# Input projections of a hybrid attention layer: six tile pairs by seven block products, kept in DRAM for the attentions

## The chip, the cores and the metric

The kernel runs on one core of a Trainium2 chip. The metric is the device time of one execution in microseconds (us). Its engines work side by side: TensorE (PE, matmuls; PEld loads its weights), VectorE (DVE), ScalarE (ACT), GpSimd (POOL), and SyncE (SP), which issues most transfers. POOL issues transfers too, on a queue of its own. Each engine executes its own instructions in order and waits for others by semaphores. On-chip memory holds tiles of 128 partitions; products land in eight banks of 512 fp32 columns.

## The reference

One layer of a streaming encoder for 1024 prompt tokens and 32 sample tokens, in fp32:

```
h   = rms_norm(x) * (1 + scale1) + shift1            # scale1, shift1 from silu(c) @ w_ada
p   = h @ w_in    # 4256 columns: q_lat 384 | c_kv 256 | k_r 32 | q_b 512 | k_b 512 | v_b 512 | g_a 1024 | g_b 1024
o_a = latent attention (softmax)       o_b = stick-breaking attention of q_b, k_b, v_b
x   = x + gate1 * rms_norm((sigmoid(g_a) * (o_a @ w_proj_a) + sigmoid(g_b) * (o_b @ w_proj_b)) @ w_out)
x   = x + gate2 * rms_norm(conv_ffn(rms_norm(x) * (1 + scale2) + shift2))
```

The change is in `p = h @ w_in` and in what stands around the stick-breaking attention. k_b and v_b are outputs as well.

## The kernel before

An fp32 product is made of three matmuls: every operand is split into a rounded part (`hi`, on ACT) and the remainder (`lo`, on DVE), and `mm3` (L71) adds high x high, high x low and low x high. `h` lies on chip for the whole first half, transposed, as `Hh` and `Hl`: eight k-tiles of 128 rows by 1056 tokens. A **projection tile** is 128 columns of `w_in` for all tokens: three blocks of 352 tokens (`BLK`), eight k-tiles, three matmuls each, 72 in all.

`stage_h` loads x and the first two ada vectors of `w_ada` in halves (`ada_half`: 8 + 8 transfers of 512 KB), normalises and transposes. `stage_sb` then takes four pairs of heads in turn (`sb_pair`): it projects the pair's q, k and v tiles (`mtile`, evacuated into `Qe`, `Qo`, `KHe`, ..., `V`), sends k and v through transposes to the outputs, and runs the attention of the pair (`sb_attend`).

The attention's order on PE, ACT and DVE is written by hand in `ORDER`, one for all pairs; the tokens are executed as they stand. `S1.0` is the score of head and row block, `a` and `e` two sigmoids on ACT, `c` the running product (DVE scan), `x` a product on DVE, `T` the transposes of one square of weights (PE), `h` and `v` their rounded and low part (ACT, DVE), `V` the product with the values (PE), `o` and `p` the sum of a result (ACT, DVE). `f` is a **fill**: one k-tile of a gate projection (three matmuls), or one k-tile of a later ada vector. The gates come from the generator in `gates`: in each pair four tiles, 4 x (24 + 2) = 104 fills; `G` sends a gate block to DRAM, `W` and `w` split the next gate weight on ACT and DVE, `D` adds an ada sum. So all 16 gate tiles lie beside the four attentions, and the 12 tiles of q, k, v between them.

`stage_lat` projects the five latent tiles and the rope key from the same `Hh`, `Hl`, and the kernel goes on with the latent attention, the merge, the up projection (already with seven block products for each pair of tiles) and the down projection.

Of the kernel before, what the change touches and what calls it, by code (L numbers as in the profile page):

```python
# [17 lines left out]
P = 128  # L18
# [25 lines left out]

class K:
# [9 lines left out]
    BUFS = {"A": 5, "Q": 3, "big": 3, "o": 2, "QZ": 1, "t": 5, "mh": 4, "ml": 4, "dh": 3, "dl": 3, "ada": 1, "G": 1, "Gs": 1, "xs": 1, "jk": 1, "s": 3, "M": 2, "pv": 1, "tr": 2, "mm": 2, "KSm": 1, "VSm": 1, "ObH": 1, "ObL": 1}  # L55
# [97 lines left out]
    def late_vectors(self):  # L153

        nc, a = self.nc, self.a
        v = self.tl(self.At, [P, TP], F32, "A")
        ps = self.bank("tr")
        dma = nc.gpsimd.dma_start
        self.rows_T(ps, v[:13, 0:P], ((0, 8, a["g_pre_ffn"][0]), (8, 3, a["g_q_lat"][0]), (11, 2, a["g_kv_lat"][0])), dma)
        for w in range(6):  # L160
            x = a["conv_w"][0, w] if w < 3 else a["conv_b"][0] if w == 3 else a["state_ffn_conv"][0, 0, w - 4]
            self.rows_T(ps[:, 44 * (w + 1) :], v[:44, P * (w + 1) : P * (w + 2)], ((0, 44, x),), dma)
        nc.vector.tensor_copy(self.gvT[:, 8:21], ps[:, :13])
        nc.vector.tensor_copy(self.cvT.rearrange("p w c -> p (w c)"), ps[:, 44 : 44 * 7])

# [22 lines left out]

    def ada_step(self, n, pool, tp, late):


        nc, a = self.nc, self.a
        ps = self.bank("mm")
        for i, (v, k) in enumerate(self.ada_todo[:n]):
            if k == 0:
                self.acc = self.tl(tp, [P, 256], F32, "ada")
                for j in range(4):
                    c = v * D + j * 256
                    nc.sync.dma_start(self.acc[32 * j : 32 * j + 32], a["b_ada"][0, c : c + 256].partition_broadcast(32))
            w = self.tl(pool, [P, D], F32, "wr")  # L200
            nc.sync.dma_start(w, a["w_ada"][0, k * P : (k + 1) * P, v * D : (v + 1) * D])
            for j in range(4):
                nc.tensor.matmul(ps[32 * j : 32 * j + 32, :256], self.cT[:, k], w[:, j * 256 : j * 256 + 256],
                                 start=i == 0, stop=i == n - 1)
            if i < n - 1:
                yield
        acc = self.acc
        late.append(lambda: nc.vector.tensor_tensor(acc, acc, ps[:, :256], ALU.add))
        del self.ada_todo[:n]
        self.ada_sum = v if k == KT - 1 else None  # L210
        yield
# [28 lines left out]
    def ada_half(self, hf, wp, tp):  # L240
# [4 lines left out]
        for k in range(KT):  # L245

            last = hf == 1 and k >= KT - 2
            w = self.tl(*((self.W, [P, 1024]) if last else (wp, [P, 2 * 512])), F32, "wr").rearrange("p (v n) -> p v n", v=2)
            nc.sync.dma_start(w, a["w_ada"][0, k * P : (k + 1) * P].rearrange("p (v h n) -> p v h n", v=6, h=2)[:, 0:2, hf])
            for j in range(4):  # L250
                c = (j % 2) * 256
                nc.tensor.matmul(ps[32 * j : 32 * j + 32, :256], self.cT[:, k], w[:, j // 2, c : c + 256],
                                 start=k == 0, stop=k == KT - 1)
        nc.vector.tensor_copy(acc, ps[:, :256])
# [8 lines left out]
        self.gain(self.g1, 1, 0, 4 * hf, 4)  # L263


    def norm_T(self, t0, xs, g, sv, tp, k0=0, k1=KT):


        nc = self.nc
        if t0 < 8:  # L270
            n = len(xs) * P
            m = 512 // n
            c = slice(t0 * P, t0 * P + n)
            for k in range(k0, k1, m):
                tr = self.bank("tr")
                f = self.tl(tp, [P, 512], F32, "hf").rearrange("p (k c) -> p k c", k=m)
                for e in range(m):
                    kc = slice((k + e) * P, (k + e) * P + P)
                    for j, x in enumerate(xs):
                        o = e * n + j * P  # L280
                        nc.tensor.transpose(tr[:, o : o + P], x[:, kc], self.idt)
                h, l = self.Hht[:, k : k + m, c], self.Hlt[:, k : k + m, c]

                both = t0 == 4 and k0 == 0
                for e in range(m):
                    for x in (f, h) if both else (f,):
                        nc.scalar.activation(x[:, e], tr[:, e * n : e * n + n], AF.Identity,
                                             bias=self.adaT[:, sv, k + e, 0:1], scale=g[:, k + e, 0:1])
                if not both:
                    nc.vector.tensor_copy(h, f)  # L290
                nc.vector.tensor_tensor(l, f, h.bitcast(F32), ALU.subtract)  # L291
        else:
            tr = self.bank("tr")
            for c in range(2):
                nc.tensor.transpose(tr[:, c * P : c * P + P], xs[0][:, c * P : c * P + P], self.idt)
            f = self.tl(tp, [P, 512], F32, "hf")[:, :256].rearrange("p (k t) -> p k t", t=TS)
            for k in range(k0, k1):
                j, c = k // 2, k % 2
                nc.scalar.activation(f[:, k], tr[:, c * P + 32 * j : c * P + 32 * j + 32],
                                     AF.Identity, bias=self.adaT[:, sv, k, 1:2], scale=g[:, k, 1:2])  # L300
            f, h, l = (x[:, k0:k1] for x in (f, self.Hht[:, :, TP:T], self.Hlt[:, :, TP:T]))
            nc.vector.tensor_copy(h, f)
            self.lo(l, f, h)
# [22 lines left out]
    def new_H(self):  # L326
        self.Hp = self.tc.alloc_tile_pool(name=self.nm("H"), bufs=1, side="right", reuse_waits="tile")
        self.Hht = self.Hp.tile([P, KT, T], F32R, name=self.nm("hh"))
        self.Hlt = self.Hp.tile([P, KT, T], F32R, name=self.nm("hl"))
        self.Hh = [self.Hht[:, k] for k in range(KT)]  # L330
        self.Hl = [self.Hlt[:, k] for k in range(KT)]

    def stage_h(self):
        nc = self.nc
        self.new_H()
        a = self.a
        with self.tc.tile_pool(name="st_h", bufs=2, reuse_waits="tile") as tp, self.tc.tile_pool(name="wada", bufs=8, reuse_waits="tile") as wp:
# [3 lines left out]
            def load(t):  # L341
                x = self.tl(wp, [P, D], F32, "x")
                nc.sync.dma_start(x, a["x_prompt"][0, t * P : (t + 1) * P])
                nc.vector.tensor_scalar(x, x, self.rstd(self.sumsq(x, P, tp, "jk0", 1024), D, P), None, ALU.mult)
                xts.append(x)

            def norm(t, hf):
                self.norm_T(t, xts[t : t + 4] if t < 8 else [xs], self.g1, 0, tp, 4 * hf, 4 * hf + 4)

            for t in range(4):  # L350
                load(t)
            self.ada_half(0, wp, tp)
            norm(0, 0)
            w = [self.w_in_tile(672)]
            for t in range(4, 8):
                load(t)
            w.append(self.w_in_tile(672 + 512))
            self.in_w = w
            norm(4, 0)
# [3 lines left out]
            self.ada_half(1, wp, tp)  # L363
            nc.vector.tensor_scalar(xs, xs, self.rstd_s(xs, tp), None, ALU.mult)
            norm(0, 1)
            norm(8, 0)
            norm(4, 1)
            norm(8, 1)


# [9 lines left out]

    BLK = ((0, NB), (NB, NB), (2 * NB, NB))
# [10 lines left out]
    def to_natural(self, f, outs, ev):  # L392

        nc = self.nc
        for t0 in (0, 4, 8):
            tr = self.bank("tr")
            n = 4 if t0 < 8 else 1
            for j in range(n):
                r = P if t0 < 8 else TS
                nc.tensor.transpose(tr[:r, j * P : j * P + P], f[:, (t0 + j) * P : (t0 + j) * P + r], self.idt)  # L400
            ev(tr, t0, n, P if t0 < 8 else TS)

    def sb_pair(self, p):
        nc, a = self.nc, self.a
        q0, k0, v0 = 672 + p * P, 672 + 512 + p * P, 672 + 1024 + p * P

        Qe = self.tl(self.Sp, [P, TP], F32R, "Q")
        Qo = self.tl(self.Sp, [P, TP], F32R, "Q")
        wh, wl = self.w_in_tile(q0)
        for c0, n, ps in self.mtile(wh, wl, self.Hh, self.Hl, self.BLK, KT):  # L410
            m = min(n, TP - c0)
            c = slice(c0, c0 + m)
            self.hi(Qe[0:64, c], ps[0:64, :m], 0.125)
            self.hi(Qo[64:128, c], ps[64:128, :m], 0.125)
            st = nc.vector.scalar_tensor_tensor
            st(Qe[64:128, c], ps[0:64, :m], 0.125, Qe[0:64, c].bitcast(F32), ALU.mult, ALU.subtract)
            st(Qo[0:64, c], ps[64:128, :m], 0.125, Qo[64:128, c].bitcast(F32), ALU.mult, ALU.subtract)
            if m < n:
                nc.scalar.mul(self.qsb[:, p], ps[:, m:n], 0.125)

        KHe = self.tl(self.Sp, [P, TP], F32R, "KH")
        KHo = self.tl(self.Sp, [P, TP], F32R, "KH")
        KLe, KLo = self.KLz
        kf = self.tl(self.At, [P, BIG], F32, "big")
        wh, wl = self.w_in_tile(k0)
# [1808 lines left out]
```

## Time and profile before

| | us |
|---|---|
| median of 3 runs (1730.93 to 1736.36) | 1733.21 |
| the profiled execution | 1733.63 |
| its span, first to last instruction | 1731.5 |
| start, until PE is full | about 0 to 45 |
| first score of the four attentions | 83.10, 199.56, 321.94, 437.15 |
| latent projections and their norms | about 530 to 620 |

A row of a group gives line, engine, operation, output<-inputs, shape, count, then busy us and the mean ns of one, then the idle time before it and what ended it. A row of the timeline gives start, length, engine, line and operation. Ends of matmuls are modelled and overlap the next ones, so their rate is read from start to start.

### The profile page before, as it was taken

How to read it: one execution, taken by the hardware profiler on the slowest of the kernel's cores; microseconds unless marked ns; L12 is line 12 of the kernel's file. 1: busy time of each engine (PE TensorE's matmuls, PEld its weight loads, DVE VectorE, ACT ScalarE, POOL GpSimd, SP SyncE). 2: the span in 40 equal slices, each digit the busy share in tenths (PEclk: the TensorE clock that was granted, in tenths of full speed). 3: DMA queues.
4: the chain of work that ended last, by engine and by line, in shares of the span. 5: the costliest groups of instructions: out<-in, count | busy, mean ns of one | idle time of the engine just before them, and what ended most of it. 6: DMA issues, size and time to landing. Idle time of an engine off the chain costs nothing. (4 is left out here: it accounts for less than half of the span.)

```text
span 1731.5 us, 29721 instructions
## 1 busy us (share of the span) xinstructions
PE 1691.4 (98%) x11518; PEld 1542.4 (89%) x11518; DVE 1207.4 (70%) x1971; ACT 911.7 (53%) x1748; POOL 283.9 (16%) x586
## 2 busy tenths in 40 slices
PE   6999999999999999999999999999999999999998
PEld 3899999999999988989889789999999999977886
DVE  4576574673663687767786679887787787778456
ACT  5454453553554666766784286444444444544442
POOL 2211110211120011101100043211111121110013
PEclk8999999999999999999999999999999999999999
DMA  8343333333342222222345531534323323697743
GB/s 322 90 132 96 108 107 97 106 113 92 112 122 68 65 65 64 75 59 68 138 143 175 184 130 37 165 104 129 129 92 128 128 92 128 212 334 248 241 147 121
DMA packets 170093, 223.62 MB, mean 129 GB/s; under 512 B 12917, under 2 KB 117056, under 8 KB 169952
## 3 DMA queue, kind: packets, MB, share of 16 engines
q1 hardware_dynamic: 154336, 177.91, 32.4%
q0 software_dynamic: 15392, 43.74, 7.1%
q8 instruction: 90, 1.47, 0.4%
q14 instruction: 51, 0.42, 0.1%
q10 hardware_dynamic: 224, 0.09, 0.0%
HBM read 169.92 MB, written 51.25 MB: 128 GB/s over the span
## 5 line engine op out<-in xcount | busy, mean ns | idle before, releaser
L65 ACT ACTIVATE wh<-wr 128x1024 fp32r<-128x1024 f32 (+6 forms) x158 | 133.8, 856 | 249.6 <-PE s L1688 78.8
L68 DVE TENSOR_TENSOR wl<-wr,wh 128x1024 fp32r<-128x1024 f32 (+5 forms) x155 | 152.7, 991 | 139.6 <-ACT wh L65 139.0
L72 PE MATMUL mm<-hh,wh 128*128 128x352 f32 x688 | 231.6, 337 | 0.0
L73 PE MATMUL mm<-hl,wh 128*128 128x352 f32 x688 | 224.2, 326 | 0.4 <-DVE hl L291 0.3
L74 PE MATMUL mm<-hh,wl 128*128 128x352 f32 x688 | 224.2, 326 | 0.0
L72 PEld LDWEIGHTS mm<-hh,wh 128*128 128x128 f32 x688 | 130.0, 189 | 9.0 <-issue 4.9
L73 PEld LDWEIGHTS mm<-hl,wh 128*128 128x128 f32 x688 | 130.0, 189 | 3.9 <-DVE hl L291 1.8
L74 PEld LDWEIGHTS mm<-hh,wl 128*128 128x128 f32 x688 | 129.7, 189 | 0.8 <-issue 0.8
L68 DVE TENSOR_TENSOR PTl<-tr,PTh 128x512 fp32r<-128x512 f32 x100 | 68.3, 687 | 50.3 <-ACT PTh L65 49.9
L1689 PE MATMUL s<-T,wl 128*128 128x256 f32 (+1 forms) x328 | 93.6, 285 | 0.0
L1687 PE MATMUL s<-T,wh 128*128 128x256 f32 (+1 forms) x328 | 93.2, 284 | 0.0
L1688 PE MATMUL s<-T,wh 128*128 128x256 f32 (+1 forms) x328 | 93.2, 284 | 0.0
L1828 DVE SCALAR_TENSOR_TENSOR u<-u,c,u 128x1058 f32<-128x1058 f32 x68 | 87.0, 1317 | 2.0 <-ACT u L1825 0.7
L65 ACT ACTIVATE PTh<-tr 128x512 fp32r<-128x512 f32 x100 | 59.4, 598 | 53.5 <-PE tr L591 50.8
L591 PE MATMUL tr<-c,A 128*128 128x128 f32 x576 | 83.6, 274 | 0.6 <-DVE A L693 0.5
L1689 PE MATMUL tr<-T,wl 128*128 128x272 f32 (+1 forms) x272 | 77.6, 285 | 0.4 <-DVE wl L68 0.4
L1687 PE MATMUL tr<-T,wh 128*128 128x272 f32 (+1 forms) x272 | 77.9, 287 | 0.0
L1688 PE MATMUL tr<-T,wh 128*128 128x272 f32 (+1 forms) x272 | 77.5, 285 | 0.0
L68 DVE TENSOR_TENSOR wl<-S,wh 128x1024 fp32r<-128x1024 f32 x40 | 48.9, 1223 | 37.4 <-ACT wh L65 36.2
L591 PEld LDWEIGHTS tr<-c,A 128*128 128x128 f32 x576 | 68.1, 140 | 5.9 <-issue 1.6
L1689 PE MATMUL mm<-T,wl 128*128 128x256 f32 (+1 forms) x256 | 73.0, 286 | 0.3 <-DVE wl L68 0.2
L1687 PE MATMUL mm<-T,wh 128*128 128x256 f32 (+1 forms) x256 | 73.1, 286 | 0.0
(694 smaller groups left out, 5391.4 us busy)
## 6 DMA issues: line engine op xcount, KB each, us to landing
wr<-in_w_ada_dram SPq DMA_DIRECT2D x48, 512.0 KB, 4.6
wr<-in_w_up_dram SPq DMA_DIRECT2D x44, 512.0 KB, 4.2
dr<-in_w_down_dram SPq DMA_DIRECT2D x43, 512.0 KB, 5.9
wr<-in_w_in_dram SPq DMA_DIRECT2D x33, 512.0 KB, 4.6
wr<-gdn SPq DMA_DIRECT2D x30, 512.0 KB, 4.2
gdn<-u POOLq DMA_DIRECT2D x23, 512.0 KB, 5.3
gd<-nat POOLq DMA_DIRECT2D x48, 176.0 KB, 2.3
t<-gd SPq DMA_DIRECT2D x16, 528.0 KB, 6.3
```

What stands on the lines that cost most here:

```text
L65: self.nc.scalar.activation(out, in_, AF.Identity, scale=scale)
L68: return self.nc.vector.tensor_tensor(out, full, hi.bitcast(F32), ALU.subtract)
L72: m(ps, lh, rh, start=start, stop=False)
L73: m(ps, lh, rl, start=False, stop=False)
L74: self.pe = m(ps, ll, rh, start=False, stop=stop).ins
L591: self.nc.tensor.transpose(tr[:, (2 * s + q) * P : (2 * s + q + 1) * P], at[q][:, b * P : b * P + P], self.idt)
L1687: m(ps[:, :n], w[0][:, k], x[0][:, k, c], start=first and k == 0, stop=False, skip_group_check=True)
L1688: m(ps[:, :n], w[0][:, k], x[1][:, k, c], start=False, stop=False, skip_group_check=True)
L1689: i = m(ps[:, :n], w[1][:, k], x[0][:, k, c], start=False, stop=k == 3, skip_group_check=True)
L1828: nc.vector.scalar_tensor_tensor(y, u[:, w : w + YW], self.cvT[:, w, cc : cc + 1], y, ALU.mult, ALU.add)
```

## The change

The 1056 tokens are held in two halves of 528 (`HC`), each half of `h` in two halves of k (four k-tiles): blocks `B11`, `B21` (first half of the tokens) and `B12`, `B22`. A pair of weight tiles then is a 2 x 2 by 2 x 2 block product, computed by seven products of four k-tiles by 528 tokens instead of eight (steps a to g), with sums of the token blocks `T1` to `T4`, which are made once, and sums of the weights, made for each pair.

1. A new stage `stage_in` runs before the attentions. It projects all 12 q, k, v tiles and four gate tiles: two pairs (q and k of the first pair of heads, two gates) by plain products (`Plain`), begun in `stage_h` while the sums of tokens are made beside them, then six pairs by seven products.
2. Results go to DRAM (`z_done`): q and k split (`qhd`, `qld`, `khd`, `kld`), v transposed and split (`vd`), gates as before (`gd`). `sb_load` brings the operands of a pair back on SP's queue; `V` has one buffer, `KLz` one per head. The block `B12` goes to DRAM in `stage_h` and comes back at the end of `stage_in`, since `T4` takes its place in between.
3. `gates` runs once for 12 tiles, three beside each attention. Blocks are 4 x 264 (`HBLK`) instead of 3 x 352, also in `stage_lat`; ada steps are 3, 3, 2 for the three tiles: 3 x 32 + 8 = 104 fills for each pair. `ORDER` is written anew.
4. `stage_h` has a written order; ACT writes the rounded `h` and the full one, where DVE cast the rounded one before. Memsets of the attention's tables go from DVE to POOL.

```diff
+class Plain:
+    def go(self, half, b, tag, part=None):
...
+        for kh in range(2) if part is None else (part,):
+            k.z_half([x[:, 4 * kh : 4 * kh + 4] for x in self.w], k.B[kh][half], b, ps, kh == 0)
+        if part != 0:
...
+            k.nc.scalar.copy(self.u[:, half * HC + c0 : half * HC + c0 + n], ps[:, :n])
...
+    Z_BLK = ((0, 256), (256, 272))
...
+    def step_a(self, g, tags):
+        w = self.unit(g["ra"][:, :512])
+        g["q1"] = self.z_q("q1", 3)
+        self.z_out(g["q1"], self.z_prod(w, self.Z["B11"], tags))
...
+    def step_d(self, g, tags):
+        X = g["X"] = self.z_prod(self.unit(g["ra"][:, :512]), self.Z["T2"], tags)
+        g["q2"] = self.tl(self.Zp, [P, HC], F32, "q2", 2)
+        self.z_out(g["q2"], X, g["q5"])
+
+    def step_e(self, g):
+        self.z_prod(self.unit(g["rb"][:, :512]), self.Z["T3"], None, g["X"])
...
+    def step_f(self, g):
+        self.z_prod(self.unit(g["rb"][:, 512:]), self.Z["T4"], None, g["X"])
...
+    def stage_in(self):
...
+        for n in range(2, len(self.PAIRS)):
+            g = self.group(n)
+            self.raw_a(g)
+            self.raw_b(g)
...
+            self.step_a(g, "s s")
...
+            self.step_b(g, "s pv")
+            self.step_c(g, "s s")
+            while self.done:
+                self.z_done(*self.done.pop(0))
+            self.out_c(g)
+            self.sums_w(g)
+            self.step_d(g, "mm mm")
...
+            self.step_e(g)
+            self.step_f(g)
...
+            self.sum_4(g)
+            self.step_g(g, "s pv")
...
+    HBLK = tuple((264 * i, 264) for i in range(4))
...
+    def sb_load(self, p):
...
+            dma(KH[lo], kh[r])
+            dma(KH[hi], kh[r])
+            dma(KL[r], kl[r])
+            dma(Q[r], qh[r])
+            dma(Q[o], ql[r])
+            ops.append((Q, KH, KL))
+            if r is lo:
+                V = self.tl(self.Sp, [P, 8, 2, P], F32R, "V", 1)
+                dma(V, self.vd[p])
...
+        f S1.0 f a1.0 S0.0 f e1.0 c1.0 f a0.0 f e0.0 f x1.0 f c0.0 f x0.0 S0.1 f G a0.1 S1.1 e0.1 f c0.1
+        a1.1 f x0.1 f W c1.1 f T0.0 S2.0a e1.1 S2.0b w f h0.0 f a2.0a f a2.0b f v0.0 e2.0a x1.1 V0.0 e2.0b G
+        c2.0a T1.1 o0 T1.0 h1.1 p0 S2.1a h1.0 x2.0a S2.1b v1.1 a2.1a v1.0 a2.1b V1.1 e2.1a c2.0b V1.0 e2.1b
...
+        T7.1 V7.2 h7.1 f T7.0 v7.1 f h7.0 f V7.1 v7.0 f2 G D V7.0 f o7 f p7 f5 G
...
-                for b, (c0, n) in enumerate(self.BLK):
+                for b, (c0, n) in enumerate(self.HBLK):
+                    if b == 2:
+                        yield from self.ada_step((3, 3, 2)[i % 3], self.W, self.At, ada)
...
+        self.fill = self.gates(range(4, 16))
```

More of the change, by code (lines that the diff above doesn't have):

```diff
@@ L194, in ada_step @@
         for i, (v, k) in enumerate(self.ada_todo[:n]):
[L195 to L201, printed above, removed]
+            w = self.ada_w.pop() if self.ada_w else self.ada_load(pool, tp, i, v, k)
             for j in range(4):
@@ L263, in ada_half @@
         self.gain(self.g1, 1, 0, 4 * hf, 4)
-    def norm_T(self, t0, xs, g, sv, tp, k0=0, k1=KT):
-        nc = self.nc
-        if t0 < 8:
[L271 to L291, printed above, removed]
```

605 lines of the change are left out of this document (443 added, 162 removed).

## The prediction

> **What bounds the kernel now.** I read the page first, then the table of busy time by stretches, then the timeline of TensorE.
>
> ```profile
> span 1731.5 us, 29721 instructions
> ...
> PE 1691.4 (98%) x11518; PEld 1542.4 (89%) x11518; DVE 1207.4 (70%) x1971; ACT 911.7 (53%) x1748; POOL 283.9 (16%) x586
> ```
>
> TensorE (PE) is busy for 98% of the span, so a stage gets shorter by what PE is spared in it, as long as nothing else takes its place. The table of stretches says where that could happen; its columns are the stretch, its length, and busy time (with instructions) of PE, PEld, DVE, ACT and POOL, then granted clock, DMA share and GB/s.
>
> ```profile
> 321.94:399.60 77.66, 77.66 (x556) 73.11 (x555) 58.02 (x89) 42.65 (x94) 14.25 (x38) 1.00 0.40 122
> 399.60:437.15 37.55, 37.53 (x238) 36.95 (x236) 11.37 (x16) 12.79 (x24) 4.14 (x6) 1.00 0.27 78
> ...
> 620.00:860.00 240.00, 235.49 (x1653) 210.12 (x1652) 180.04 (x444) 169.89 (x422) 33.59 (x58) 1.00 0.23 71
> ...
> 1050.00:1506.00 456.00, 454.90 (x3793) 447.20 (x3792) 367.64 (x542) 222.37 (x362) 91.62 (x206) 1.00 0.36 119
> ```
>
> The first row is one stick-breaking attention (the third pair) with its four gate tiles beside it, the second the three projections q, k, v of the next pair. Both are full of PE work at clock 1.00. In the attention VectorE (DVE) works 58.02 of 77.66 us (75%). The third row, most of the latent attention, has DVE at 75% too, and PE idles 1.9%; the fourth, the up projection, which already uses seven block products, has DVE at 81% and PE idles 0.2%. So 75 to 81% of DVE can go with a full PE, and can cost 2%.
>
> **What a matmul costs.** Ends are modelled and overlap, so I count from start to start: 26 rows of 352 columns (first and last shown), 12 rows of 264, four transposes up to the next start, and, from the chain of waits, two marks three up-projection pairs apart.
>
> ```profile
> 399.88 0.33 PE L72 MATMUL mm<-hh,wh 128*128 128x352 f32 x1
> ...
> 403.96 0.32 PE L73 MATMUL mm<-hl,wh 128*128 128x352 f32 x1
> ...
> 645.38 0.29 PE L72 MATMUL mm<-ObH,wh 128*128 128x264 f32 x1
> ...
> 646.72 0.29 PE L74 MATMUL mm<-ObH,wl 128*128 128x264 f32 x1
> ...
> 394.22 0.60 PE L591 MATMUL tr<-c,A 128*128 128x128 f32 x4
> 394.57 0.72 PE L605 MATMUL pv<-ptd,V 128*128 128x256 f32 x4
> ...
> 1179.67 1.43 PE pv L1965 x24
> 1242.77 1.43 PE pv L1965 x24
> ```
>
> 352 columns: 4.08 us / 25 = 0.163 us. 264 columns: 1.34 / 11 = 0.122 us. Both are 0.46 ns a column, so a width of 264 carries no price of its own. A transpose of 128 columns takes 0.35 / 4 = 0.088 us, 0.028 more than that rate; such a floor exists, but below 264. A projection tile is 72 matmuls of 352: 11.75 us; two tiles are 23.5. A pair of tiles by seven block products takes (63.10 - 1.43) / 3 = 20.56 us.
>
> **The change part by part.**
>
> *Block products.* Six pairs (12 tiles) go from 23.5 to 20.56 us each: 6 x 2.94 = **-17.7 us**. Four tiles stay plain, in blocks of 256 and 272: 4 x 96 x 0.122 = 46.9 against 47.0, nothing. Their evacuation, the transposes to natural layout, the ada steps (32 in all before and after) and the late vectors are the same PE work, elsewhere.
>
> *Widths.* Twelve gate tiles and the latent tiles go from three blocks of 352 to four of 264: 96 x 0.122 against 72 x 0.163, nothing. By the Trainium skill, "TensorE: Matmul & The Clock Gate", section "Back-to-back issue gap", a stream of weight loads and matmuls takes 81 ns at 128 columns and 131 ns at 512, which has a large fixed part per matmul; the two rows above (0.163 and 0.122 us, proportional to the width) do not agree, and I go by the rows. The 504 more matmuls would cost about 32 us by the page's fixed part of 64 ns, an estimate from its two figures.
>
> *Start.* The first 60 us are no full PE:
>
> ```profile
> 35.00:40.00 5.00, 5.00 (x32) 2.99 (x30) 1.67 (x4) 3.72 (x7) 0.00 (x0) 0.71 0.58 224
> 40.00:45.00 5.00, 4.58 (x54) 2.53 (x53) 1.43 (x4) 0.24 (x2) 0.82 (x4) 1.00 0.00 2
> ...
> 43.08 1.50 PE L252 MATMUL s<-wr,cT 128*32 128x256 f32 x24
> ...
> 46.16 1.45 ACT L287 ACTIVATE hf<-tr,c,c 128x512 f32<-128x512 f32 x2 [5.93 <-DVE c L236]
> ...
> 56.10 1.18 ACT L299 ACTIVATE hf<-tr,c,c 128x32 f32<-128x32 f32 x4
> ...
> L73 PE MATMUL mm<-hl,wh 128*128 128x352 f32 x16 | 7.0, 435 | 0.4 <-DVE hl L291 0.3
> L72 PE MATMUL mm<-hh,wh 128*128 128x352 f32 x16 | 6.5, 409 | 0.0
> L74 PE MATMUL mm<-hh,wl 128*128 128x352 f32 x16 | 6.1, 378 | 0.0
> L72 PE MATMUL s<-hh,wh 128*128 128x352 f32 x14 | 4.6, 329 | 0.0
> L73 PE MATMUL s<-hl,wh 128*128 128x352 f32 x14 | 4.5, 323 | 0.0
> L74 PE MATMUL s<-hh,wl 128*128 128x352 f32 x13 | 4.3, 330 | 0.0
> ```
>
> Before, 89 projection matmuls of 352 (31.3 thousand columns) have started by 60 us. The new first stage issues 120 plain matmuls of 256 or 272: 31.3 thousand as well. The last ada weights have landed by 40 us (DMA share 0.00 behind it), but PE takes them at 43.08; the new order puts them ahead of the projections, which could bring the second half of the ada vectors 2 us earlier. Against it ScalarE (ACT) now writes both the rounded and the full value, 16 activations of 1.45 / 2 = 0.72 us after that point, with 2 x 1.18 for the sample and 3 copies: about 15 us from 44, so 59 to 60. I take **0**, bounds -4 (ada early, ACT never late) and +4 (PE held in the written order).
>
> *The new stage.*
>
> ```profile
> L68 DVE TENSOR_TENSOR wl<-wr,wh 128x1024 fp32r<-128x1024 f32 x4 | 4.8, 1212 | 2.8 <-ACT wh L65 2.8
> ...
> L208 DVE TENSOR_TENSOR ada<-ada,mm 128x256 f32<-128x256 f32 x4 | 1.7, 417 | 0.2 <-PE mm L203 0.2
> ```
>
> The sums of the tokens are eleven passes over two halves of 1056 columns (differences and low parts), at about 1.25 us (1.21 for 1024): 27 us of DVE beside 46.9 us of plain products; the plain tiles are their cover, and without it the first T2 product would wait. Within a group the same two banks are read by DVE between the products with T2, T3 and T4, with one bank's 12 matmuls (1.47 us) as cover for a read of 0.42 (the second row) plus whatever DVE is in, up to 1.2. The up projection has the same shape and lost 0.2%. Four such places in six groups: **+1.5**, bounds 0 and 5.
>
> *Spill and reload.* q, k, v go to DRAM and come back on SP's queue. Nothing of PE in that, but V has one buffer, so the load of the next V waits for the last value product, and behind it on SP stand the second head's operands and the next gate weight.
>
> ```profile
> wr<-in_w_up_dram SPq DMA_DIRECT2D x44, 512.0 KB, 4.2
> ...
> 20.00:25.00 5.00, 2.51 (x19) 1.56 (x19) 2.97 (x8) 3.23 (x4) 0.00 (x0) 0.93 1.05 404
> ```
>
> Behind that point lie 1.05 + 1.31 + 0.52 = 2.9 MB: 7.1 us at 404 GB/s, and 2.9 more to land (512 KB take 4.2, of which 1.3 at that rate): 10.0 us. The gate weight is split (W, on ACT) 19 fills later, with scores of 1.3 us and switches of about 0.5 between them: 19 x 0.366 + 1.8 = 8.8 us. ACT would wait 1.2 us; PE has six more fills and the scores S2.0 in hand before it needs ACT's h0.0. **+1** over three boundaries, bounds 0 and 8. The first attention has a like entry: its operands can only come when T3 and T2 are free, some 6 us before the stage ends. **+1**, bounds 0 and 5.
>
> *The attentions with three gate tiles.* Each loses one tile: 77.66 - 11.75 = 65.9 us of PE work. What fills DVE there:
>
> ```profile
> L68 DVE TENSOR_TENSOR PTl<-tr,PTh 128x512 fp32r<-128x512 f32 x12 | 8.2, 687 | 7.6 <-ACT PTh L65 7.6
> ...
> L68 DVE TENSOR_TENSOR ptd<-tr,ptd 128x384 fp32r<-128x384 f32 x8 | 4.4, 550 | 0.3 <-ACT ptd L65 0.2
> ...
> L579 DVE TENSOR_TENSOR o<-pv,o 64x256 f32<-64x256 f32 x7 | 2.9, 421 | 3.0 <-ACT o L577 2.9
> ...
> L544 DVE TENSOR_TENSOR A<-A,M 128x320 f32<-128x320 f32 x4 | 1.9, 486 | 0.3
> ...
> L463 DVE TENSOR_TENSOR V<-nat,V 128x512 fp32r<-128x512 f32 x2 | 1.4, 679 | 0.0
> ...
> L462 DVE CAST V<-nat 128x512 fp32r<-128x512 f32 x2 | 0.8, 425 | 7.9 <-ACT nat L440 7.9
> ...
> L577 ACT COPY o<-pv 64x256 f32<-64x256 f32 x7 | 2.6, 368 | 3.5 <-PE pv L605 3.4
> ```
>
> DVE loses one weight split (1.2) and the value split (2.2): 54.6 of 65.9, 83%, a little over the highest row of before. There are still 104 fills, but each is 0.366 instead of 0.49 us, and the new order has spots without any. Between V0.0 and V1.1 PE has seven transposes and four score products of 384: 0.6 + 0.7 = 1.3 us. In that time ACT must copy o0 (0.37) and DVE must do p0, x2.0a and v1.1 (0.42 + 0.49 + 0.55): 1.83 us in a row. PE waits 0.5 us, and 0.2 more before V1.0, whose low part takes 0.69. Four pairs: **+3**. Bounds: 0.5 (0.2% of 264 us) and 10 (twice 1.9%).
>
> **The sum** is -17.7 + 0 + 1.5 + 1 + 1 + 3 = -11.2 us. The profiled execution took 1733.6 us (2.1 outside the span), the median of the runs 1733.2; from the median: **1722.0**. What this kernel's measurement can tell from no change is about 0.3%, 5.2 us.
>
> **The rivals.**
>
> 1. *All of it stays* (0.15): the fills are dense enough, the boundaries hidden, ada early. 1733.2 - 17.7 = 1715.5, down to 1711.5. For it: PE idles nothing in the attention row. Against: DVE at 83%, and the spot worked out above.
> 2. *Given back at the boundaries* (0.12): the loads behind V and the first operands come late. At 4 us for each of three boundaries and the entry, -17.7 + 16 with the 4.5 of the new stage and the attentions: 1736. For it: 10.0 us of loads against 8.8. Against: a DMA share of 0.40 on average.
> 3. *The attention becomes a chain of DVE and ACT* (0.11), slower than before: the gate tile taken out was cover, and the pair does not shrink by 11.75 us. Point of decision: 17.7 / 4 = 4.4 us of waits a pair, a pair over 70.3 us. If a pair takes 72, +24 - 17.7 + 3.5 = 1743; if it stays at 77.66, 1766. For it: four dependent steps (scan, product, low part, sum) share one engine at 83%. Against: 81% with a full PE in the up projection.
> 4. *A fixed price per matmul* (0.02): the floor of 0.028 us seen at 128 columns holds for each of the 504 further matmuls, 14.1 us: 1736. That is the page's kind of rule. Against: the rows at 352 and 264.
> 5. The change not doing what it says has no room of its own: the number of matmuls is in the code, and if the sums of the tokens come late it looks like rival 2.
>
> **How the numbers follow.** The forecast has 0.60, its own range 1714 to 1730. The range of 1711 to 1738 takes in rivals 1, 2 and 4 and the forecast with its bounds, and leaves out most of rival 3. Faster (under 1728): 0.55 of the forecast and rival 1, 0.70. Within 0.3%: 0.05, 0.10 of rival 2, 0.02: 0.17. Slower: 0.11 and the tail of rival 2: 0.13.
>
> **What will show it.** Six groups of 168 matmuls at 20.6 us each, from the first q1 to the last (right: under 125 us with PE idle under 3). An attention pair of 66 to 67 us by the start of its first score and its last value product; DVE at 80 to 83% in it. The wait rows of PE should name DVE's low part of PT and the DMA of V or the gate weight at the pair's start with under 1 us each. If PE waits for M, A or PT sum to over 18 us, rival 3 is right; if waits for KH, Q, V or W's raw weight do, rival 2. I would be wrong from the start if PE's plain products begin to run full only after 64 us.

## The result and the profile after

The kernel after takes 1762.6 us (median of 4 runs, 1761.14 to 1764.98) against 1733.9 us before (4 runs on the same chip): a ratio of 1.0168, 95% interval 1.0147 to 1.0188. It is **slower**, by 28.7 us, where 11.2 us less were forecast.

From the page of after, its span and the busy time of each engine:

```profile
span 1759.9 us, 31441 instructions
...
PE 1691.3 (96%) x12184; PEld 1540.8 (88%) x12184; DVE 1260.4 (72%) x2083; ACT 928.5 (53%) x1804; POOL 300.3 (17%) x622
```

PE is busy as long as before, 1691 us, although six pairs need an eighth fewer products. Either the products are no cheaper, or PE spends the gain elsewhere. The stretches of after tell which. The first five rows lie between the starts of the `T1` products of two successive groups of `stage_in`, the last two between the first scores of two successive pairs of heads. A row gives the stretch, its length, the busy time (with instructions) of PE, PEld, DVE, ACT and POOL, then granted clock, DMA share and GB/s.

```profile
107.59:130.50 22.91, 21.64 (x176) 21.23 (x176) 20.04 (x31) 7.80 (x15) 3.00 (x2) 1.00 0.40 115
130.50:158.74 28.24, 24.50 (x188) 24.03 (x187) 16.67 (x33) 9.84 (x21) 10.35 (x16) 0.94 0.50 170
158.74:180.41 21.67, 21.67 (x179) 21.46 (x178) 13.21 (x22) 7.85 (x15) 5.45 (x9) 1.00 0.51 168
180.41:208.45 28.04, 24.10 (x180) 23.69 (x178) 13.99 (x24) 7.33 (x18) 5.03 (x7) 0.88 0.36 117
208.45:232.21 23.76, 22.89 (x189) 22.42 (x187) 13.97 (x27) 9.23 (x18) 9.30 (x15) 1.00 0.61 199
253.71:331.77 78.06, 71.45 (x554) 65.01 (x555) 54.73 (x86) 39.69 (x91) 14.06 (x39) 0.93 0.82 235
331.77:402.06 70.29, 69.97 (x572) 63.67 (x571) 54.22 (x86) 41.74 (x96) 13.14 (x37) 1.00 0.66 194
```

The third group runs without a gap at clock 1.00 in 21.67 us. The second and fourth take 28 us: PE stands 3.7 and 3.9 us and then works at half clock (0.94 and 0.88 are means). The first attention loses 6.6 us to idle and has clock 0.93, the second loses 0.3. So the loss comes in lumps. What PE waited for between 45 and 270 us (engine, line, releaser: sum, times, longest), and then the same stops in PE's timeline:

```profile
PE tr L741 <- ACT nat L743: 5.6, 3, 3.7
PE mm L550 <- DVE u L560: 3.9, 1, 3.9
PE s L816 <- DMA Q<-qld: 2.2, 1, 2.2
PE mm L550 <- DVE q L560: 1.3, 1, 1.3
```

```profile
145.36 0.28 PE L741 MATMUL tr<-c,u 128*32 128x128 f32 x1 [3.74 <-ACT nat L743]
...
198.81 0.59 PE L550 MATMUL mm<-b12h,wh 128*128 128x272 f32 x1 [3.87 <-DVE u L560]
...
253.71 0.41 PE L816 MATMUL s<-KH,Q 128*128 128x384 f32 x1 [2.16 <-DMA Q<-qld]
...
273.35 1.08 PE L245 MATMUL mm<-wr,cT 128*32 128x256 f32 x8 [5.59 <-DMA wr<-in_w_ada_dram]
```

The first two rows name ACT and DVE, but those engines only pass a wait on. Their own timelines, ACT and then DVE:

```profile
144.72 1.26 ACT L743 COPY nat<-tr 128x512 f32<-128x512 f32 x2 [5.95 <-DMA out_dram<-nat]
```

```profile
192.04 0.42 DVE L560 TENSOR_TENSOR u<-mm,q 128x256 f32<-128x256 f32 x1 [0.97 <-PE mm L550]
196.99 0.69 DVE L569 TENSOR_TENSOR s<-S 128x512 f32<-128x512 f32 x1 [4.53 <-DMA S<-in_w_in_dram]
197.72 0.69 DVE L589 TENSOR_TENSOR S<-S,S 128x512 f32<-128x512 f32 x1
198.33 0.43 DVE L560 TENSOR_TENSOR u<-mm,q 128x272 f32<-128x272 f32 x1
```

Until 144.72 ACT waits 5.95 us for a store to free one of two buffers (`nat`). At 192 DVE does one of two evacuations of a bank pair (L560), then stands at `sum_1` (L569) of a *later* group, two ahead (n = 7, "pair seven" below, while PE works on n = 5), whose weights land only at 197; the second evacuation, on which PE waits, is queued behind it. And after each stop the clock is low:

```profile
192.00:197.00 5.00, 2.94 (x25) 2.73 (x23) 0.43 (x2) 1.15 (x2) 0.00 (x0) 0.99 0.79 248
197.00:200.00 3.00, 1.19 (x5) 1.19 (x6) 2.97 (x6) 0.00 (x0) 0.00 (x0) 0.50 0.00 0
200.00:203.00 3.00, 3.00 (x16) 3.00 (x15) 1.33 (x3) 0.00 (x0) 0.00 (x0) 0.50 0.00 0
203.00:206.00 3.00, 3.00 (x23) 3.00 (x23) 0.71 (x2) 0.41 (x1) 0.00 (x0) 0.89 0.00 0
206.00:209.00 3.00, 3.00 (x27) 3.00 (x26) 2.05 (x4) 1.47 (x4) 0.00 (x0) 1.00 0.00 0
```

From 200 to 203 PE is full, yet starts 16 matmuls where the last row has 27. The mean clock over the span is 0.987, against 0.996 before: 1759.9 x 0.013 less 1731.5 x 0.004 is 16 us of clock lost, an estimate, about as much as six pairs were to spare PE, so its busy time did not fall. The Trainium skill, "TensorE: Matmul & The Clock Gate", section "What's actually happening", says that an idle window of about 3.4 us halves the clock until PE has been busy for such a window. These rows agree in part: 3.87 us idle, then 0.50 up to 203; but PE is idle from 195 and the clock is 0.50 from 197 on, 2 us into the stop.

**Where the 39.6 us between forecast and fact lie.** Forecast span: 1731.5 - 11.2 = 1720.3; fact: 1759.9. The marks are the first score and the last sample product (before: 526.58, after: 552.92).

```profile
526.58 0.43 PE L720 MATMUL pv<-A,vsb 32*128 32x64 f32 x2
```

```profile
552.92 0.43 PE L1054 MATMUL pv<-A,vsb 32*128 32x64 f32 x2
...
624.41 0.68 PE L1205 MATMUL mm<-big,c 128*128 128x264 f32 x2 [1.80 <-DVE big L1342]
```

| | forecast | fact | over |
|---|---|---|---|
| until the first score: 83.10 + 3 x 37.55 + 4 x 11.75 - 17.7 = 225.0, + 0 + 1.5 + 1 | 227.5 | 253.7 | 26.2 |
| four attentions: 526.6 - 83.1 - 112.7 - 47.0 = 283.8, + 3 + 1 | 287.8 | 299.2 | 11.4 |
| all that follows, 28.4 - 26.3 (a wait of 1.80 at 624.41 among it) | 0 | 2.0 | 2.0 |

Behind the attentions the distance to before is not constant: 29.4 us at the first score of the latent attention (616.73 and 646.08), 26.5 at the last matmul, 28.4 at the end.

### The profile page after: what moved, and what is told of

Same layout as the page of the kernel before. It is cut to its first block, busy times and chain, and to the rows that moved or that the text cites. A ratio compares the mean times of both kernels' runs of the same rounds, so it can differ in the third digit from the quotient of the medians.

```text
span 1759.9 us, 31441 instructions
## 1 busy us (share of the span) xinstructions
PE 1691.3 (96%) x12184; PEld 1540.8 (88%) x12184; DVE 1260.4 (72%) x2083; ACT 928.5 (53%) x1804; POOL 300.3 (17%) x622
## 5 line engine op out<-in xcount | busy, mean ns | idle before, releaser
L103 PE MATMUL mm<-H,wh 128*128 128x264 f32 x348 | 102.6, 295 | 0.0
L105 PE MATMUL mm<-H,wl 128*128 128x264 f32 x348 | 99.9, 287 | 0.0
L104 PE MATMUL mm<-H,wh 128*128 128x264 f32 x348 | 99.6, 286 | 0.0
L99 DVE TENSOR_TENSOR wl<-S,wh 128x1024 fp32r<-128x1024 f32 (+1 forms) x58 | 60.9, 1056 | 35.5 <-ACT wh L96 35.4
L96 ACT ACTIVATE wh<-S 128x1024 fp32r<-128x1024 f32 (+1 forms) x58 | 53.4, 926 | 45.7 <-PE s L2028 13.4
L886 DVE TENSOR_TENSOR_SCAN M<-M,tab 128x512 f32<-128x512 f32 (+4 forms) x64 | 58.6, 916 | 21.2 <-ACT M L871 21.0
L2028 PE MATMUL mm<-T,wh 128*128 128x272 f32 (+1 forms) x256 | 72.8, 285 | 0.0
```

The costliest lines, as they stand in the source:

```text
L96: self.nc.scalar.activation(out, in_, AF.Identity, scale=scale)
L99: return self.nc.vector.tensor_tensor(out, full, hi.bitcast(F32), ALU.subtract)
L103: m(ps, lh, rh, start=start, stop=False)
L104: m(ps, lh, rl, start=False, stop=False)
L105: self.pe = m(ps, ll, rh, start=False, stop=stop).ins
L886: self.nc.vector.tensor_tensor_scan(r, r, tab[:, ::-1], 0.0, ALU.mult, ALU.max)
```

## The experiments

**Theory:** the seven products cost what was forecast; PE loses time where an engine's queue stands at an instruction that waits for a transfer, and in the half clock behind each stop. **Rivals:** (A) the transfers as a whole are the bound, so a stop that is removed comes back at the next one; (B) the hand-offs between seven products are dear in themselves; (C) the attention is bound by DVE and ACT; (D, E) the start is bound by loads, or its written order is the better one. Each run is compared by the time of its first score (after: 253.71), which e6, with nothing changed ahead of it, has at 253.21 and e3, where only the reload just ahead of it is left out, at 254.81: less than about 1.5 us there means nothing. The first `T1` product dates the start: 107.59 in after, 106.83, 107.03, 107.81 and 107.92 in e1, e3, e6 and e7, whose start is the same.

| run | first score | span | median, ratio to before |
|---|---|---|---|
| after | 253.71 | 1759.9 | 1762.6, 1.0168 |
| e1_sum_late | 246.21 | 1756.2 | 1758.3 (one run) |
| e2_no_rows | 243.16 | 1750.3 | 1752.2 (one run) |
| e3_no_reload | 254.81 | 1754.7 | 1756.5 (one run) |
| e4_start_free | 251.45 | 1761.6 | 1763.7 (one run) |
| e5_plain | 251.96 | 1752.3 | 1754.2 (one run) |
| e6_ada_later | 253.21 | 1754.3 | 1756.4 (one run) |
| e7_fills_first | 254.49 | 1761.3 | 1763.4 (one run) |
| e8_all | 240.08 | 1745.1 | 1747.2, 1.0072 (1.0045 to 1.0099) |
| e9_squares_first | 251.14 | 1757.9 | 1760.0 (one run) |
| e10_all_squares | 242.48 | 1746.9 | 1749.3, 1.0083 (1.0063 to 1.0103) |
| e11_plain_start | 251.51 | 1753.1 | 1752.5, 1.0093 (1.0071 to 1.0114) |
| e12_dve_copies | 250.67 | 1756.3 | 1758.8 (one run) |
| e13_turn_sooner | 251.56 | 1757.0 | 1759.1 (one run) |
| e14_all_written | 241.71 | 1743.4 | 1747.1, 1.0087 (1.0059 to 1.0115) |

### One stop at a time: e1, e2

```diff
+        with self.tc.issue_after(self.zf) if g["n"] > 2 else ExitStack():
+            self.nc.vector.tensor_tensor(s, g["rb"][:, :512], g["rb"][:, 512:], ALU.add)
```

(`zf` is the last evacuation of `step_f` of the group ahead.)

> Edit: the first sum of weight halves of each later pair (DVE, L569) may not be issued before the last evacuation of the pair ahead of it. Theory (the six products themselves cost what was forecast; the time is lost where an engine's queue, which runs in order, stands at an instruction that waits for a transfer, and in the half clock after such a stop): the 4.53 us that DVE stands at that sum for the weights of pair seven, with PE idle 3.87 us at L550 behind it, goes, and the slow clock after it; of the stop at 145 us only DVE's part goes. First score 6 to 9 us earlier (245 to 248 instead of 253.7), span 1751 to 1754. Rival A (the transfers as a whole are the bound of this stage, so a stop that is taken away comes back at the next transfer): first score within 2 us of 253.7, span 1758 to 1760. Rival B (hand-offs between products are dearer than forecast, no single stop matters): no change either, and the groups between the stops longer than 21.7 us.

First score 7.5 us earlier, the theory's number. The fourth group of e1:

```profile
179.11:200.84 21.73, 21.67 (x179) 21.46 (x178) 13.18 (x24) 7.25 (x15) 4.50 (x6) 1.00 0.45 147
```

It takes 21.73 us instead of 28.04, so 6.3 of the 7.5 are this stop; 0.8 is there at the first `T1` product already. The stop at pair seven is gone, and the one at 144 us stays (3.26 us). Rivals A and B fall for this stop: nothing came in its place. The span gave back 4 us of it much later, 3 of them in a spell told of at the end.

```diff
-            nc.gpsimd.dma_start(dst, st[:q].rearrange("r (j c) -> r j c", j=n))
```

> Edit: the stores of the turned rows of k and v to the outputs are left out, so those outputs are not written. Theory: ACT's 5.95 us wait at L743 for a store to free a buffer goes, and with it PE's 3.74 us idle at L741 and the 3 us of half clock after it; the stop at pair seven stays unless the freed queue lets its weights land sooner. First score 5 to 6 us earlier without that, 10 to 12 with it; span 1748 to 1755. Rival A (transfers as a whole are the bound): with 0.9 MB less to store the whole stage speeds up, first score more than 10 us earlier and DMA share near 1.0 still. Rival B (hand-offs): under 2 us.

First score 10.6 us earlier. The second group of e2, then the first 2 us behind its stop at pair seven:

```profile
128.25:152.49 24.24, 23.52 (x189) 22.62 (x187) 16.10 (x33) 9.84 (x21) 6.05 (x10) 1.00 0.43 153
```

```profile
191.06:193.00 1.94, 1.94 (x9) 1.94 (x10) 1.94 (x4) 0.00 (x0) 0.00 (x0) 0.56 0.00 0
```

The stop at L741 is gone: 24.24 us instead of 28.24, so 4.0 of the 10.6 are this stop. The one at pair seven shrinks from 3.87 to 2.37 us, since its weights come sooner (2.1), and the wait for Q from 2.16 to 0.61; 2.3 us are there at the first `T1` product already. So the stops share the queues. Rival A expected more than 10 us too, but with a DMA share near 1.0; it is 0.31 to 0.47 over the groups of e2, and the group in between still takes 21.67 us, so the transfers do not bind the stage as a whole.

### The first attention: e3, e6, e7

```diff
-                self.B12 = self.two(self.Hp, "b12")
-                for d, x in zip(self.b12d, self.B12):
-                    nc.gpsimd.dma_start(x, d.bitcast(F32R))
+                self.B12 = Z["T4"]
```

> Edit: the quarter of the input operand that the fourth block operand overwrote is not loaded again, so the gate products of the second token half read other numbers. Theory: the 2.2 MB of that load crowd the queues just as the first attention's loads and the ada weights are wanted; without it the 5.97 us that PE waits for the ada weights (L245) shrink to under 1.5 us and the half clock after it goes; the wait for Q at the entry (2.16 us) shrinks too. Pair one from 78.1 to 68 to 71 us, first score at most 3 us earlier, span 1747 to 1753. Rival A (the first attention's own loads, V, K and Q of two pairs, fill the queues by themselves): pair one stays over 75 us. Rival C (the attention is bound by DVE and ACT beside the longer fills): pair one stays at 78 and DVE's share does not fall.

```diff
-                    if b == 2:
+                    if b == (2 if i else 3):
                         yield from self.ada_step((3, 3, 2)[i % 3], self.W, self.At, ada)
```

(with the first `D` and the third `G` of `ORDER` exchanged in the first attention)

> Edit: in the first attention the three ada products of the first gate tile come eight fills later (the third block of the tile first), everything is loaded and computed as in after. Theory: only the place of that wait is wrong, the ada weights land at about 273 and the fills that come first take some 4 us at the first attention's pace, so the 5.97 us wait shrinks to under 2 us and no half clock follows; pair one 70 to 73 us instead of 78.1, span 1752 to 1756. Rival A (the jam stops whichever fill comes next): the third block of the tile waits for the reloaded operand instead, pair one stays over 76 us.

The first attention's stretch in e3, then in e6 (in after: 78.06 us, clock 0.93):

```profile
254.81:324.75 69.94, 69.14 (x555) 63.61 (x555) 54.08 (x83) 39.70 (x91) 14.03 (x39) 0.98 0.82 232
```

```profile
253.21:324.87 71.66, 69.53 (x554) 63.40 (x555) 54.55 (x86) 39.81 (x91) 14.05 (x39) 0.98 0.88 256
```

Both come out as the theory said. Without the reload the ada weights are in time; with it, the same ada products eight fills later wait only 0.8 us for them (and the third block 1.0 for the reload), and the pair takes 71.7. DVE's 54 us of work is the same in all three: rival C falls. The entry's wait for Q did not shrink without the reload (2.32 us), a miss of the expectation.

```diff
-        f S1.0 f a1.0 S0.0 f e1.0 c1.0 f a0.0 f e0.0
+        f5 S1.0 a1.0 S0.0 e1.0 c1.0 a0.0 e0.0
```

> Edit: in the first attention five fills come ahead of the first score instead of one, and four fewer between it and the multiply. Theory: 1.5 us of the 2.16 us wait for Q are covered and the half clock after it goes: pair one's last V product 2 to 4 us earlier, span 1756 to 1758. Rival C (DVE and ACT set the attention's pace, so a later first score only moves the waits into it): no change or up to 2 us slower.

No gain: the first score waited 0.90 us instead of 2.16, but the fills were then ahead of their ada weights, and PE stood 2.44 and 3.89 us there. The time is rival C's, the cause another: while the queues are full, covering one load uncovers the next.

### The products themselves: e5

```diff
-            self.step_a(g, "s s")
...
+            for c0 in self.PAIRS[n]:
+                X = Plain(self, c0)
+                X.split()
...
+                for i, tag in enumerate(("s", "s", "mm", "pv")):
+                    X.go(i // 2, i % 2, tag)
```

> Edit: the six later pairs are made by plain products, eight block products of 132 KB operands a pair instead of seven, with no weight sums; nothing is overwritten, so nothing is loaded again. All else is as after. Theory (seven products cost 20.6 us a pair, plain ones 23.5; what the seven save is lost again in stops that the sums and the reload make): PE without its two long stops between 100 and 250, pairs of about 24.6 us with the turns of their rows, the stop for the ada weights under 1.5 us; first score 248 to 256, pair one near 70, span 1748 to 1760, so that the products bring nothing as they stand. Rival A (transfers bound the stage whatever the products): stops remain at the stores of turned rows, first score 258 to 266, span over 1760. Rival B (hand-offs of the seven-product scheme are its price): first score under 245.

Two stretches of e5, and its first attention:

```profile
100.00:150.00 50.00, 49.95 (x411) 49.32 (x410) 17.95 (x21) 14.84 (x31) 11.44 (x23) 1.00 0.68 201
100.00:250.00 150.00, 149.86 (x1228) 148.20 (x1227) 38.18 (x42) 46.32 (x93) 33.43 (x58) 1.00 0.60 185
...
251.96:319.64 67.68, 67.36 (x556) 62.16 (x555) 54.44 (x86) 39.94 (x92) 15.78 (x43) 1.00 0.61 171
```

Plain products leave no gap, though they move *more* bytes in the stage (201 GB/s between 100 and 150 against 117 in after): rival A falls for the stage. Rival B does not hold here either: it asked for a first score under 245. One pair of q and k tiles, from mark to mark in PE's timeline of e5:

```profile
161.93 0.29 PE L550 MATMUL pv<-b12h,wh 128*128 128x272 f32 x1
...
186.50 0.29 PE L550 MATMUL pv<-b12h,wh 128*128 128x272 f32 x1
```

24.57 us, against 21.67 for the like group of after: seven products save 2.90 us a pair, where 2.94 was forecast. And e5 dates the loss of the start. Without block products and without stops its first score should come at 83.10 + 112.7 + 47.0 = 242.8; it comes at 251.96. So **9.2 us are lost ahead of 100 us**.

### The start: e4, e9, e12, e13

```diff
-            with tc.manual_schedule(engines={E.PE, E.Activation, E.DVE}):
+            if True:
```

> Edit: the order of the start (normalization, ada products, first plain products) is not held as written, the scheduler orders it. Theory (the written order puts the second half's ada products behind turns of x that wait for x to be scaled, and what is late there is late until 66 us): second half's operand ready earlier, the first plain products done 4 to 7 us earlier, span 1753 to 1756. Rival D (the start is bound by the loads of x and of the ada weights, whatever the order): within 2 us of 1759.9. Rival E (the written order is the better one): later than after by more than 3 us.

2.3 us at the first score, less than the 4 to 7 expected; the written order is a part of the loss.

```diff
-                each(n, n, n, n)
-                A.go(0, 0, "mm", 0)
                 for t in range(4, 8):
+                    each(n)
                     scale(t)
+                A.go(0, 0, "mm", 0)
```

> Edit: in the written order of the start the squares and the scaling of the second four x tiles (ACT L136, DVE L414) stand between the four steps of the first normalization instead of behind all of them; nothing else moves. Theory (ACT's queue, with two passes for each turned tile where before had one, delays the squares to 29 us, and PE idles 4.2 us for them between 31 and 36 and runs at half clock after that): the scaled tiles come 2 to 4 us sooner, PE idles under 2 us there, the second half's ada products end by 46 instead of 48.35, first score 2 to 4 us earlier, span 1756 to 1758. Rival D (the loads of x and of the second ada half land no sooner, so the idle time moves to the ada products): first score within 1 us of 253.7.

2.6 us, as the theory said: PE turns the second half's ada sums (L302) at 45.64 instead of 47.48. At the first `T1` product e4 is at 104.88 and e9 at 105.99: 2.7 and 1.6 us ahead of after. The two gains do not add: with both edits e10 is at 106.11.

```diff
-                put(H[0][:, k, c], x, q)
+                if hf:
+                    nc.vector.tensor_copy(H[0][:, k, c], f)
+                else:
+                    put(H[0][:, k, c], x, q)
```

> Edit: as e9_squares_first, and in the second half's normalization DVE copies the high half from the first pass (eight copies) where ACT made a second pass over the turned tile (eight of 0.67 us). Theory A (in the second half ACT's sixteen passes, 10.7 us where before had eight, are what PE waits for between 46 and 70): those passes end 3 to 5 us sooner than the 65 us of after, first score 2 to 4 us ahead of e9_squares_first (247 to 249). Theory B (the place of the turns in PE's written order is what ACT waits for): first score within 1 us of 251.1.

```diff
-                each(norm(8, 0), n)
+                each(norm(8, 0), n, n)
```

> Edit: as e9_squares_first, and the fourth turn of the second half's first normalization stands ahead of the products of A's fourth block (pv) in the written order instead of behind them. Theory B (ACT waits 2.62 us at 53.5 for that turn, which stands on PE behind products that wait for DVE and run at half clock): ACT's gap goes, its passes end 2 to 3 us sooner, first score 1 to 3 us ahead of e9_squares_first (248 to 250). Theory A (ACT's sixteen passes bound it): under 1 us.

Neither moved the first score by 1 us (250.67 and 251.56 against 251.14), so neither ACT's doubled passes nor the place of that one turn is the cause by itself. The stretches of e9, then of e12:

```profile
45.00:50.00 5.00, 3.44 (x27) 2.85 (x25) 2.83 (x6) 3.41 (x7) 0.00 (x0) 1.00 0.24 46
50.00:55.00 5.00, 4.32 (x22) 4.09 (x22) 2.69 (x7) 2.08 (x5) 0.00 (x0) 0.66 0.93 354
...
60.00:65.00 5.00, 4.60 (x40) 4.38 (x37) 4.93 (x11) 4.65 (x10) 0.00 (x0) 1.00 0.00 0
```

```profile
45.00:50.00 5.00, 4.66 (x36) 3.99 (x34) 3.16 (x9) 2.27 (x6) 0.00 (x0) 1.00 0.07 9
50.00:55.00 5.00, 3.91 (x31) 3.77 (x32) 4.25 (x11) 1.70 (x3) 0.00 (x0) 1.00 1.02 371
...
60.00:65.00 5.00, 3.64 (x30) 3.23 (x28) 4.89 (x10) 2.32 (x6) 0.00 (x0) 1.00 0.00 0
```

With ACT relieved, PE gains 0.8 us of work and a full clock by 55, and loses 1.0 us again behind DVE, which is full from 60 to 65 in both. The first 100 us of before, then of e5:

```profile
0.00:100.00 100.00, 82.41 (x555) 66.18 (x556) 55.77 (x113) 51.67 (x97) 24.10 (x54) 0.95 0.58 200
```

```profile
0.00:100.00 100.00, 76.29 (x581) 61.32 (x582) 50.95 (x92) 54.86 (x92) 17.20 (x36) 0.91 0.63 221
```

PE idles 23.7 us in e5 and 17.6 in before: 6.1 of the 9.2, and 4.7 of these behind 45 us (PE busy 50.08 of 55, against 54.73). The other 3.1 stand beside the lower clock. No edit here took more than some 2 to 4 us off; what makes the rest, some 5 to 7, stays open.

### All together: e8, e10, e14, and e11

> Edit: the weight sum held back, three buffers for the turned rows instead of two, the start ordered by the scheduler, the ada products later and the fills first, all of it together; nothing is left out. Theory (the losses are separate and add up): 7.5 us for the sum, 3 to 5 for the rows, 2.3 for the start, 5 to 8 for the ada products, 1 to 4 for the fills, 19 to 27 us in all until the latents; median 1736 to 1745, within 0.7% of the kernel before. Rival A (one bound by transfers under all of them): under 12 us together, median over 1750.

The groups of e8, to be held against the five of after:

```profile
126.65:151.49 24.84, 23.23 (x188) 22.57 (x187) 15.28 (x32) 9.57 (x20) 9.94 (x15) 1.00 0.54 192
151.49:173.18 21.69, 21.69 (x180) 21.48 (x178) 14.94 (x25) 8.45 (x18) 6.44 (x10) 1.00 0.52 172
173.18:194.91 21.73, 21.66 (x179) 21.46 (x178) 13.19 (x24) 7.25 (x15) 4.49 (x6) 1.00 0.44 147
194.91:218.65 23.74, 23.16 (x189) 22.48 (x187) 15.04 (x28) 9.44 (x19) 9.46 (x16) 1.00 0.60 193
```

No group has low clock any more, and the second takes 24.84 us instead of 28.24 with its third buffer; first score 13.6 us earlier, last sample product 19.6 (533.3), at the low end of what was expected, and the median, 1747.2, just above it. The losses add up to that low end, and the kernel is still 0.7% slower than before. In its first attention (71.73 us) PE now waits 2.65 us for the reload, which e6's rival A had expected.

> Edit: as e8_all, with the fills of the first attention in their old places and the squares of the second four x tiles between the steps of the first normalization, in the scheduler's order. Theory: the start gains another 1 to 3 us and the first attention 1 to 2; median 1740 to 1745. Rival D (the start is bound by loads once the order is free) and Rival C (the fills' place does not matter): median 1746 to 1749. Either way it stays over the kernel before, since the latents' 2 us, the start's rest and the spell of half clock near 780 are not touched.

> Edit: as e10_all_squares, with the start in the written order (the scheduler's order made the squares' new place worth nothing: 242.48 against 240.08). Theory: first score 240 to 242, the first attention without its stop for ada weights, median 1743 to 1748. If the start's written order is worse than the scheduler's even so: median over 1749.

> Edit: as e5_plain, with the scheduler's order in the start and the squares of the second four x tiles between the steps of the first normalization. Theory: the start gains what it gains with the seven products, 2 to 5 us; median 1748 to 1753, so that the seven products with their stops taken away (e10) are worth 6 to 11 us more than plain ones. Rival B (what the seven products save is taken by their hand-offs): e10 and e11 within 3 us of each other.

e10 is no better than e8, as rival D had it: under the scheduler's order the new place of the squares is worth nothing. e14, with the written start, has the shortest span (1743.4; its profiled run lacks the spell of 3 us told of at the end, which e8 and e10 have) and the same median. Its stop for ada weights is gone as expected (0.5 us), but PE waits 2.80 us for the reload there. e8, e10 and e14 can't be told apart, and none beats the kernel before. e11 has plain products and e10 seven: 9.0 us at the first score, but 6.4 at the latents, since e10's first attention is 3.8 us longer (71.5 us, it has the reload), and 3.2 between the medians, whose intervals overlap. The 6 to 11 were expected of the medians, so that was a miss, and rival B, with its 3 us, is not excluded at the end of the kernel. Nor did the start of e11 gain its 2 to 5 us: its first score is 0.45 us ahead of e5's. With two stops taken away the seven products are worth some 6 us at the latents, a third of the 17.4 that PE is spared.

## Why the prediction was wrong

- **Six pairs, -17.7: right.** 2.90 us by the pair that can be compared, 17.4 for six. The sign given for it was "under 125 us with PE idle under 3"; the six take 148 us (102.81 to 250.90). It was the wrong sign, for the products were as cheap as forecast while PE idled over 10 us between them.
- **A price per matmul by width: none,** as taken (rival 4, and with it the fixed part in the Trainium skill, "TensorE: Matmul & The Clock Gate", section "Back-to-back issue gap"). 168 products and nine transposes in 21.67 us leave no room for it.
- **Start, 0 with bounds -4 and +4: failed.** Lost 9.2 us. The term compared the amounts of work and one date (ada 2 us earlier). It did not follow the written order through PE: turns behind turns that wait for scaled x, which waits for squares behind ACT's doubled passes (e9: 2.6 us at the first score), with PE held in that order (e4: 2.3; the two do not add). The ada sums came later than before, not sooner (47.48 against 45.13). The greater part of the loss has no cause shown. The sign set for this, PE full only after 64 us, came true in the main: PE is busy throughout from 55 to 65, at clock 0.81 and then 1.00, idles 0.88 us more at 67 and then runs full to 81.
- **The new stage, +1.5 with bounds 0 and 5: failed, the largest step.** The fact is 26.2 + 2.5 - 9.2 = 19.5 us with the entry. The term asked only what a bank's hand-over costs, by the up projection's 0.2%. It had no row for what is queued *in front of* the evacuation on DVE and ACT: a sum of weights not yet landed (6.3 us by e1), and copies into two buffers that a store must free (4.0 by e2). The 2.16 us for Q and many waits of up to 1.3 us, not told apart, make the rest. The half clock, 1.3 to 2.4 us of PE's busy time a stop (second group 24.50 against 23.23 in e8, fourth 24.10 against 21.67 in e1), was in no term. The up projection was no model: it has no stores of turned rows.
- **Three boundaries, +1: held.** PE waits in pairs two to four are at most 1.0 us each, all for DVE and none for a transfer.
- **The entry, +1 with bounds 0 and 5: the kind was right, its reach was not.** PE waits 2.16 us for Q, but behind the attention's operands stand the ada weights, with 2.2 MB of reload beside them on another queue: 5.97 us of waits and half clock, 8.1 us by e3, 6.4 by e6.
- **The attentions, +3 by DVE: right in the sum.** With e5's first attention, in which nothing stops PE, the four take 67.68 + 552.92 - 331.77 = 288.8 us against 287.8. PE's waits for DVE in pairs two to four are 2.4 us, of which 1.8 in the sample products, so the place worked out for them does not show. From its first score to its last value product the second pair takes 396.35 - 331.77 = 64.6 us against the 66 to 67 given as a sign (seven fills now stand behind that product), with DVE at 54.22 us against 54.6. Rival 3 falls; that its 1766 lies near the measured time is chance.

```profile
396.35 0.28 PE L939 MATMUL pv<-PTl,V 128*128 128x256 f32 x1
```

- **The rivals.** Rival 2 named the right kind of cause, transfers that come late, but at the boundaries and the entry alone, with 16 us; the same cause inside `stage_in` and in the first attention was not in any case, and so the range ended at 1738.

## What to carry to other kernels

Before a stage gets new transfers or sums, list for each engine's queue what stands in front of the instruction that frees the busy engine, and when its operand lands: an early sum was worth 6.3 us and copies into two buffers 4.0 here, each more than a pair of tiles saves (2.90). Price a stop with the half clock that can stand behind it: 3.87 us of idle PE cost 6.3. And do not take a full stage as a model for another by its engine shares: compare what its queues wait for.

## What the runs showed of the hardware

Stops shorter than 3.4 us can have half clock behind them too. In e1 the stop of 3.26 us has 0.50 behind it, in e2 that of 2.37 has 0.56 (row above), in e8 the 2.65 us at the reload has 0.50, from 1.5 us behind it on; in e14 2.80 us at the reload has 1.00 throughout. What decides between these is not shown.

A spell of half clock can come without a stop. Between 765 and 795 us both rows below run the same stage, e1 some 8 us ahead of after, and PE has no idle time of 0.9 us in either. After, then e1:

```profile
770.00:775.00 5.00, 5.00 (x28) 3.18 (x26) 3.44 (x8) 3.82 (x7) 0.00 (x0) 1.00 0.26 69
775.00:780.00 5.00, 4.50 (x37) 4.06 (x34) 4.74 (x10) 2.58 (x9) 0.00 (x0) 1.00 0.49 159
```

```profile
770.00:775.00 5.00, 4.29 (x32) 3.66 (x32) 4.52 (x14) 3.18 (x10) 0.00 (x0) 1.00 0.34 125
775.00:780.00 5.00, 4.76 (x34) 4.01 (x32) 3.34 (x8) 3.49 (x10) 0.00 (x0) 1.00 0.02 7
780.00:785.00 5.00, 5.00 (x26) 4.39 (x26) 1.01 (x6) 1.35 (x4) 1.12 (x2) 0.73 0.19 55
785.00:790.00 5.00, 5.00 (x28) 4.97 (x29) 0.69 (x1) 2.00 (x6) 0.00 (x0) 0.59 0.32 85
```

The spell costs e1 2.9 us and e8 3.3. e1, e2, e4, e5, e6, e8, e10 and e11 have it in their profiled run, after, e3, e7, e9, e12, e13 and e14 have not. So 3 us of a gain can vanish 500 us later for no reason in the code, and gains of this size are better read at the stage than at the end. By the Trainium skill, "TensorE: Matmul & The Clock Gate", section "What's actually happening", the window runs free of the kernel, so that the position in time would decide; no run here shows that by itself, and the page's condition, an idle window, was not met.
